# Half of g_attn moved from the attention's fill into the seven products behind it, softmax sums formed there, and new pacing constants

## The chip, the cores and the metric

The kernel runs on one core of a Trainium2 chip. The metric is the device time of one execution in microseconds (us). The engines named below are PE (matrix products), PEld (its weight loads), DVE (vector), ACT (scalar and activation functions), POOL (GpSimd) and SP (which issues most DMAs here). Each engine runs its own instructions in order and waits for the others by semaphores.

## The reference

One decoder block over 1040 positions (16 meta tokens and 1024 tokens), float32, 8 heads of 64:

```python
h = rmsnorm(x, norm_g)
proj = h @ w_in   # split: u_pool 512, z_pool 512, q, k, v 512 each, z_attn 512, f_logit 8, g_pool 1024, g_attn 1024
y_pool = causal_multiscale_pool(u_pool, pool_w, pool_scale) * silu(z_pool)
y_attn = forgetting_attention(q, k, v, log_sigmoid(f_logit + b_forget)) * silu(z_attn)
merged = sigmoid(g_pool) * (y_pool @ w_up_pool) + sigmoid(g_attn) * (y_attn @ w_up_attn)
out = rmsnorm(x + merged @ w_out, final_norm_g)   # only the 1024 tokens are returned
```

`forgetting_attention` is a causal softmax of `q k / 8` plus the summed log gates between key and query, times `v`.

## The kernel before

**Precision.** Matrix operands are kept as a high and a low part (`hh`/`hl` of the normed input, `whi`/`wlo` of weights). A product is three: high by high, high by low, low by high. Scores take two (L678, L679: `qa` and `ql` against `ka`), values two (L740: `ph` and `pl`, the parts of the probabilities). One half-chunk of a plain projection (128 columns by 512 tokens, 8 blocks of the contraction) is thus 24 matmuls of 128x512, all recorded at L170.

**Stages.** The input is normed and the first head pair's q, k, v are formed. Then comes the attention, then z_attn and z_pool, then the two up-projections with their gates, then the output product and the last norm.

**Attention.** Sixteen units follow each other: head pair p, head e, query half. A unit has 512 queries; with the first half it has 5 key blocks of 128 (units 0, 2, ... 14), with the second 9 (units 1, 3, ... 15). Per key block `qk` writes a score bank `ps` in PSUM (L678, L679), of which two exist; ACT empties it to `S` with the key's gate as bias (L687), DVE the masked part on the diagonal (L685), and DVE keeps the running maximum `pt` (L692; for the first block ACT copies it, L690). `maxes` then finds each query's maximum over the 128 partitions: transpose (L697), reduce (L702), two rounds of small ACT copies between partitions (L704, L707) with DVE maxima (L705, L708), and a transpose back (L710). `soft` handles a key block: DVE subtracts the maximum (L719), ACT takes the exp (L720) and rounds it to `ph` (L723), DVE forms the rest `pl` (L724), POOL adds the exps of all blocks up in `acc` (L732). `av` (L740) multiplies with V, two blocks behind. `finish` stores the unit's values; there DVE also transposes `acc` (L755) and reduces it (L757) to the sums of the softmax, which SP stores.

**Order.** The score products of the next unit are merged with the softmax of the present one (`merged`). Between them PE gets fill: projections that nothing in the attention waits for (u, the 8 chunks of g_pool, the 8 of g_attn, each chunk two half-chunks) and those that the next head pair wants (q, k, v). `F.pull(ns)` takes as many matmuls off the fill's list as fit into ns. How much is pulled is set by constants: behind each step `PACE` times an assumed DVE time less the step's PE time, `LM1` and `LM2` in `maxes`, and `LATENCY` ahead of each of a unit's last two value products.

```python
656:                yield w, 1.04 * w + 70, 2 * mm_ns(w), (lambda b=b: self.qk(b))
661:                yield w, 1.75 * w + 130, 2 * mm_ns(w), (lambda b=b: self.soft(b))
768:        for _, (w, dve, pe, f) in sorted(out_, key=lambda t: t[0]):
769:            f()
770:            F.pull(max(0.0, PACE * dve - pe))
```

So PE's order is that of the program text with the fill put in by these numbers. On the other engines a scheduler orders the instructions of this stage by what they depend on. What is left of the fill behind the last value product is done by `F.drain()` (L829). The evicted fill goes from PSUM through `st` (L342) to DRAM (`spill`) and returns for the gates.

**The seven products.** z_attn and z_pool are one product of the normed input with 1024 columns of `w_in`, done in the manner of Strassen: the input is cut in two token halves and two halves of the contraction, the weights in two halves of the contraction and the two column halves z_attn and z_pool. Seven products of block sums (512 by 512 by 512) replace eight. Each has four groups of 128 columns, each group is 12 matmuls (`g_prod`, L973). The block sums of the weights, `GS`, and of the input, `HS`, are made in DRAM during the attention: `put` (L586) is an SP DMA that copies, `add` a POOL DMA that accumulates, placed at units by the table `SUMS`. The first product's weights `graw` are loaded at unit 13 and rounded to `gw0` by ACT at unit 14 (L821), POOL forms the low part. In the product stage (manual order, `M2`) `w_split` makes the high part of each weight block on ACT (L953) and the low on POOL (L136) or DVE; `keep`, `plus_` and `silu` empty the banks on ACT and DVE. The up-projections (`up`) read the gates back from `spill` and take their sigmoid; the output product (L1232) is of the same kind as the seven.

## Time and profile before

| | us |
|---|---|
| median of 3 runs | 727.25 (726.98 to 727.72) |
| profiled execution | 727.18 |
| its span on the core | 725.5 |
| norm and first q, k, v (to the first score product) | 83.2 |
| attention (to the last value product) | 377.2 |
| rest of the fill | 12.6 |
| seven products | 82.0 |
| up-projections with gates | 87.0 |
| output product and last norm | 83.5 |

The stages are windows of the profiled execution, from 0 to 83.20, 460.40, 473.00, 555.00, 642.00 and 725.50 us. A row of the windows view gives for a stretch its length, the busy time of each engine with the number of instructions, the granted TensorE clock (1.00 is full), the DMA share and GB/s. A row of the timeline gives start, duration, engine, line, operation, result<-operands, shape, and in brackets how long the engine stood idle just before and what it waited for. A row of the chain of waits gives start, length and line of a piece of the work that ended last. A row of the groups (line, engine, operation, tiles, shape, count) gives busy time and mean ns of one, then the idle time ahead of them. In the list of PE's waits stand the tile and line that waited, what released it, and the sum, the number and the longest of the waits.

### The profile page before, as it was taken

Reading aid. Unit: us, or ns where it says so; the run is one execution under the profiler, and the core shown is the slowest. Engines: PE = TensorE matmul, PEld = TensorE weight load, DVE = VectorE, ACT = ScalarE, POOL = GpSimd, SP = SyncE. Lnnn points to the kernel's source line nnn. Section 1 sums busy time; section 2 is a strip of 40 time slices with the busy share of each in tenths; the row PEclk is TensorE's granted clock in tenths of the full one; section 3 lists DMA queues with packets and bytes.
Section 4 is the critical chain, followed back from the end, with each engine's and each line's share of the span. In section 5 each row is a group of like instructions: output and inputs, shape, how many; then the busy total and the mean of one; then the engine's idle time right before and its main releaser. Section 6 shows DMA issues by size and latency. Waiting matters only on the chain.

```text
span 725.5 us, 10804 instructions
## 1 busy us (share of the span) xinstructions
PE 712.8 (98%) x3637; PEld 613.8 (85%) x3637; DVE 506.9 (70%) x913; ACT 422.4 (58%) x930; POOL 330.8 (46%) x409
## 2 busy tenths in 40 slices
PE   8999999999999999999999999999999999999996
PEld 6997999998888898898888878888888888888885
DVE  5753577667688676886768658765877545888775
ACT  6652577557686677676765576252776423525445
POOL 5412236639446584463653666493843010006152
PEclk9999999999999999999999999999999999999998
DMA  9201124782984868838576599486906267761006
GB/s 307 63 26 34 29 84 166 175 262 60 295 201 95 222 173 221 218 90 222 104 202 148 156 265 248 126 301 202 293 12 238 93 219 248 248 245 59 0 2 232
DMA packets 88506, 119.40 MB, mean 165 GB/s; under 512 B 11297, under 2 KB 54305, under 8 KB 86450
## 3 DMA queue, kind: packets, MB, share of 16 engines
q1 hardware_dynamic: 84896, 99.83, 43.0%
q0 software_dynamic: 2256, 16.25, 12.4%
q10 hardware_dynamic: 1298, 2.63, 1.0%
q8 instruction: 28, 0.46, 0.3%
q14 instruction: 28, 0.23, 0.1%
HBM read 92.81 MB, written 53.67 MB: 202 GB/s over the span
## 4 chain that ended last, share of the span: by engine, by line
PE 84%; ACT 3%; DVE 2%; DMA 1%; POOL 1%; issue 1%; POOLq 0%; ACTq 0%; DVEq 0%
PE pj L170 53%; PE pj L1232 8%; PE pj L973 8%; PE po L740 5%; PE pt L973 3%; PE pt L1232 2%; PE ps L679 2%; PE ps L678 2%; PE pj L515 1%; DMA graw<-in_w_in_dram 1%; POOL acc L732 1%; ACT S L687 1%; DMA raw<-in_w_in_dram 1%; ACT S L720 1%; PE pj L300 0%
## 5 line engine op out<-in xcount | busy, mean ns | idle before, releaser
L170 PE MATMUL pj<-hh,whi 128*128 128x512 f32 (+3 forms) x640 | 144.9, 352 | 0.0
L170 PE MATMUL pj<-hh,wlo 128*128 128x512 f32 (+3 forms) x640 | 143.2, 350 | 0.3 <-POOL wlo L434 0.3
L170 PE MATMUL pj<-hl,whi 128*128 128x512 f32 (+3 forms) x640 | 141.9, 350 | 0.0
L158 POOL TENSOR_TENSOR wlo<-raw,whi 128x256 fp32r<-128x256 f32 x116 | 90.7, 826 | 84.4 <-ACT whi L156 33.1
L170 PEld LDWEIGHTS pj<-hh,whi 128*128 128x128 f32 x640 | 108.0, 188 | 12.1 <-ACT hh L223 0.5
L170 PEld LDWEIGHTS pj<-hl,whi 128*128 128x128 f32 x640 | 108.1, 188 | 12.0
L170 PEld LDWEIGHTS pj<-hh,wlo 128*128 128x128 f32 x640 | 108.0, 188 | 12.0 <-POOL wlo L434 0.5
L724 DVE TENSOR_TENSOR pl<-S,ph 128x512 fp32r<-128x512 f32 (+4 forms) x112 | 83.5, 756 | 26.6 <-ACT ph L723 25.7
L732 POOL TENSOR_TENSOR acc<-acc,S 128x272 f32<-128x272 f32 (+4 forms) x80 | 74.4, 930 | 14.5 <-ACT S L720 9.3
L692 DVE TENSOR_TENSOR pt<-pt,S 128x400 f32<-128x400 f32 (+2 forms) x96 | 46.8, 487 | 44.7 <-ACT S L687 43.1
L687 ACT ACTIVATE S<-ps,negc 128x400 f32<-128x400 f32 (+2 forms) x96 | 48.5, 514 | 37.0 <-DVE S L685 33.0
L136 POOL TENSOR_TENSOR gw<-graw,gw 128x256 fp32r<-128x256 f32 x40 | 45.5, 1173 | 29.8 <-ACT gw L953 12.2
L723 ACT ACTIVATE ph<-S 128x512 fp32r<-128x512 f32 (+4 forms) x112 | 52.7, 479 | 9.6 <-PE po L740 9.2
L720 ACT ACTIVATE S<-S 128x512 f32<-128x512 f32 (+4 forms) x112 | 49.8, 478 | 13.3 <-DVE S L719 13.2
L719 DVE TENSOR_TENSOR S<-S,pt 128x512 f32<-128x512 f32 (+4 forms) x112 | 50.7, 498 | 0.6
L1125 DVE TENSOR_TENSOR rl<-pj,rl 128x512 f32<-128x512 f32 x32 | 22.0, 690 | 28.7 <-PE pj L170 28.4
L973 PE MATMUL pj<-gh,gw 128*128 128x512 f32 x180 | 42.0, 389 | 0.0
L156 ACT ACTIVATE whi<-raw 128x512 fp32r<-128x512 f32 x58 | 33.8, 622 | 11.6 <-DMA raw<-in_w_in_dram 5.1
L973 PEld LDWEIGHTS pj<-gh,gw 128*128 128x128 f32 x180 | 33.8, 188 | 7.1
L678 PE MATMUL ps<-qa,ka 128*128 128x512 f32 (+4 forms) x112 | 36.5, 326 | 3.2 <-ACT S L687 3.2
L679 PE MATMUL ps<-ql,ka 128*128 128x512 f32 (+4 forms) x112 | 37.5, 335 | 0.0
L740 PE MATMUL po<-pl,V 128*128 128x512 f32 (+4 forms) x112 | 37.4, 334 | 0.0
(229 smaller groups left out, 1304.7 us busy)
## 6 DMA issues: line engine op xcount, KB each, us to landing
raw<-in_w_in_dram SPq DMA_DIRECT2D x31, 512.0 KB, 5.2
gs<-in_w_in_dram SPq DMA_DIRECT2D x5, 1024.0 KB, 9.9
td<-in_w_out_dram SPq DMA_DIRECT2D x5, 1024.0 KB, 8.4
xt<-in_x_dram SPq DMA_DIRECT2D x8, 512.0 KB, 7.4
sp_gp<-st SPq DMA_DIRECT2D x16, 256.0 KB, 4.6
gs<-gs POOLq DMA_DIRECT2D x4, 1024.0 KB, 9.1
td<-td POOLq DMA_DIRECT2D x4, 1024.0 KB, 11.3
sp_ga<-st SPq DMA_DIRECT2D x16, 256.0 KB, 4.4
```

The lines of the kernel that those rows point to most:

```text
L158: ins = nc.gpsimd.tensor_tensor(lo[:, k:k + 2], raw[:, k:k + 2], r32(hi[:, k:k + 2]), op=ALU.subtract)
L170: nc.tensor.matmul(ps, a, b, start=(i == 0), stop=(i == len(seq) - 1))
L678: nc.tensor.matmul(ps[:kb, c0:], ka[:, k0:k0 + kb], qa[:, q0 + c0:q0 + 512], start=True, stop=False)
L679: nc.tensor.matmul(ps[:kb, c0:], ka[:, k0:k0 + kb], ql[:, q0 + c0:q0 + 512], start=False, stop=True)
L687: nc.scalar.activation(s[:kb, f0:], ps[:kb, f0:], AF.Identity, bias=nb_)
L720: exps.append(nc.scalar.activation(s[:kb, c0:], s[:kb, c0:], AF.Exp))
L723: nc.scalar.activation(ph[:kb, c0:], s[:kb, c0:], AF.Copy)
L724: dves.append(nc.vector.tensor_tensor(pl[:kb, c0:], s[:kb, c0:], r32(ph[:kb, c0:]), op=ALU.subtract))
L732: accs.append(nc.gpsimd.tensor_tensor(acc[:kb, c0:], acc[:kb, c0:], s[:kb, c0:], op=ALU.add))
L740: nc.tensor.matmul(self.po[:, c0:], v, r[:kb, c0:], start=(b == 0 and i == 0), stop=(b == self.nb - 1 and i == 1))
L973: nc.tensor.matmul(ps, op_w[n][p][k // 2][:, k % 2, i * 128:(i + 1) * 128], op_h[n][q][k // 2][:, k % 2], start=start and m == 0, stop=m = ...
L1232: nc.tensor.matmul(ps, pick(A_, k, p)[:, i * 128:(i + 1) * 128], pick(B_, k, q)[:, c0:c1], start=start and n == 0, stop=n == 11, skip_grou ...
```

## The change

Chunks 4 to 7 of g_attn leave the fill. Chunks 4 and 5 are put beside z_attn, 6 and 7 beside z_pool, so that the column halves of the seven products are 768 wide in place of 512: six groups for each product, 42 in place of 28. The block sums `GS` become 512x768, each copied by two DMAs (`put_g`).

The weight blocks are now loaded in pairs of 128 columns (`pair_in`), and `w_split` makes one group's operand at a time: ACT the high part, and the low part POOL in two pieces for two groups of three and DVE in one for the third. A table `order` lists the 42 groups, and `before`/`extra` say what other work stands at which group. `evict` empties the banks; the new gate chunks are put together in two tiles `XE` and stored to `spill` as the others are (`g_store`, `g_flush`). Chunks 6 and 7 come out with the other sign, which `up` takes into its sigmoid by a scale of -1.

The sums of the softmax: `finish` no longer transposes and reduces `acc`; SP stores the whole `acc` (128x512, 256 KB a unit) to `accd`. In the product stage `acc_in` loads two units at a time and `acc_sum` transposes and reduces 1024 columns, eight times.

The pacing constants change as well: `PACE`, the assumed times of the steps, `LM2`, and `TAIL` in place of `LATENCY` ahead of a unit's last two value products.

```diff
-PACE = 1.67
+PACE = 1.0
 LATENCY = 1800.0
-LM1, LM2 = 1400.0, 3200.0
+LM1, LM2 = 1400.0, 1800.0
+TAIL = 900.0
...
+accd = dr.tile([128, 16, 512], F32, name="accd")
-GS = {n: dr.tile([512, 512], F32, name=f"gs{n}") for n in (1, 2, 3, 4, 5)}
+GS = {n: dr.tile([512, 768], F32, name=f"gs{n}") for n in (1, 2, 3, 4, 5)}
+def put_g(dst, src):
+    put(dst[:, :512], src[0])
+    put(dst[:, 512:], src[1])
...
-yield w, 1.04 * w + 70, 2 * mm_ns(w), (lambda b=b: self.qk(b))
+yield w, 1.05 * w + 165 + 300 * (b * KB + KB > self.t0), 2 * mm_ns(w), (lambda b=b: self.qk(b))
-yield w, 1.75 * w + 130, 2 * mm_ns(w), (lambda b=b: self.soft(b))
+yield w, 2.6 * w + 376, 2 * mm_ns(w), (lambda b=b: self.soft(b))
...
-at = ap_.tile([KB, 512], F32, name="mt")
-after(nc.vector.transpose(at, acc), dves[-1])
-r = sm.tile([128, 16], F32, name="sr")
-nc.vector.tensor_reduce(r, at.rearrange("p (j b) -> p j b", b=32), axis=AX.X, op=ALU.add)
-nc.sync.dma_start(sums[4 * self.p + 2 * self.e + self.half], r)
+nc.sync.dma_start(accd[:, 4 * self.p + 2 * self.e + self.half], acc)
...
-raws = [(n, j) for n, c in (("gp", 8), ("ga", 8)) for j in range(c)]
+raws = [(n, j) for n, c in (("gp", 8), ("ga", 4)) for j in range(c)]
...
-    F.pull(LATENCY)
+    F.pull(TAIL)
     u.av(b)
...
+def acc_in(k):
+    nc.sync.dma_start(zp[k % 2].rearrange("p (u c) -> p u c", u=2), accd[:, 2 * k:2 * k + 2])
+def acc_sum(k):
+    at = zp[2 + k % 2]
+    sall = XE[1][:, 0, :256].rearrange("p (u j) -> p u j", j=16)
+    nc.vector.transpose(at, zp[k % 2])
+    nc.vector.tensor_reduce(sall[:, 2 * k:2 * k + 2].rearrange("p u j -> p (u j)"),
+                            at.rearrange("p (j b) -> p j b", b=32), axis=AX.X, op=ALU.add)
...
+def w_split(e):
+    n, i = e
+    raw = raw_w[n, "aabbgg"[i]][:, :, 128 * (i % 2):][:, :, :128]
+    op = bp.tile([128, 2, 4, 128], F32R, name="gw", tag="y", bufs=6)
+    op_w[e] = op
+    nc.scalar.activation(op[:, 0], raw, AF.Copy)
+    if splits[0] % 3 == 2:
+        nc.vector.tensor_tensor(op[:, 1], raw, r32(op[:, 0]), op=ALU.subtract)
+    else:
+        for k in (0, 2):
+            nc.gpsimd.tensor_tensor(op[:, 1, k:k + 2], raw[:, k:k + 2], r32(op[:, 0, k:k + 2]), op=ALU.subtract)
+    splits[0] += 1
...
+order = [(n, i) for n in range(7) for i in {5: (3, 2, 1, 0, 4, 5), 6: (4, 5, 3, 2, 1, 0)}.get(n, range(6))]
...
+for x, e in enumerate(order[:38]):
+    if x == 0:
+        g_prod(order[0])
+        g_prod(order[1])
+    if 4 <= x + AH < 42:
+        split_next(order[x + AH])
+    if x + 2 < 38:
+        g_prod(order[x + 2])
+    for f in before.get(e, ()):
+        f()
+    if x:
+        evict(order[x - 1])
...
-    ins = nc.scalar.activation(sg_, sg_, AF.Sigmoid)
+    ins = nc.scalar.activation(sg_, sg_, AF.Sigmoid, scale=-1.0 if a and j > 5 else 1.0)
```

How this moves instructions is shown at three places. In these rows a line number is that of the program they belong to: the fill is L170 before and L171 after, the score products are L678 and L679 before, L691 and L692 after; `pj` is a bank of the fill, `ps` a score bank. The first place is PE from the last fill ahead of unit 9 to its first score product; of before:

```order
L300 MATMUL pj_3359<-ident_93,vt_3044 128x128 x4
L170 MATMUL pj_3383<-hh0_119,whi_3374 128x512 x4
L170 MATMUL pj_3383<-hh1_121,whi_3374 128x512 x4
L170 MATMUL pj_3383<-hl0_120,whi_3374 128x512 x4
L170 MATMUL pj_3383<-hl1_122,whi_3374 128x512 x4
L170 MATMUL pj_3383<-hh0_119,wlo_3375 128x512 x3
L678 MATMUL ps_3437<-qa_2363,ka_2528 128x512
```

The same place on PE after the change, from unit 8's last value product on (`po` with `ph` and `pl` is L753 there):

```order
L753 MATMUL po_3004<-ph_3189,V_1911 128x16
L753 MATMUL po_3004<-pl_3190,V_1911 128x16
L171 MATMUL pj_3225<-hh1_121,whi_3216 128x512 x3
L171 MATMUL pj_3225<-hl0_120,whi_3216 128x512 x4
L171 MATMUL pj_3225<-hl1_122,whi_3216 128x512 x4
L171 MATMUL pj_3225<-hh0_119,wlo_3217 128x512 x4
L691 MATMUL ps_3280<-qa_2279,ka_2452 128x512
```

Between unit 8's last score product and unit 9's first stand 23 matmuls of fill in place of 36; between those of units 6 and 7, 25 in place of 39.

The second place is PE from unit 9's first to its fourth score product; of before:

```order
L170 MATMUL pj_3383<-hh0_119,wlo_3375 128x512
L170 MATMUL pj_3383<-hh1_121,wlo_3375 128x512 x4
L170 MATMUL pj_3458<-hh0_119,whi_3374 128x512 x4
L678 MATMUL ps_3463<-qa_2363,ka_2528 128x512
L679 MATMUL ps_3463<-ql_2364,ka_2528 128x512
L170 MATMUL pj_3458<-hh1_121,whi_3374 128x512 x2
L678 MATMUL ps_3471<-qa_2363,ka_2528 128x512
L679 MATMUL ps_3471<-ql_2364,ka_2528 128x512
L170 MATMUL pj_3458<-hh1_121,whi_3374 128x512 x2
L170 MATMUL pj_3458<-hl0_120,whi_3374 128x512
L678 MATMUL ps_3479<-qa_2363,ka_2528 128x512
L679 MATMUL ps_3479<-ql_2364,ka_2528 128x512
```

The same place after the change:

```order
L171 MATMUL pj_3225<-hh1_121,wlo_3217 128x512 x4
L171 MATMUL pj_3300<-hh0_119,whi_3216 128x512 x3
L691 MATMUL ps_3304<-qa_2279,ka_2452 128x512
L692 MATMUL ps_3304<-ql_2280,ka_2452 128x512
L171 MATMUL pj_3300<-hh0_119,whi_3216 128x512
L691 MATMUL ps_3311<-qa_2279,ka_2452 128x512
L692 MATMUL ps_3311<-ql_2280,ka_2452 128x512
L171 MATMUL pj_3300<-hh1_121,whi_3216 128x512
L691 MATMUL ps_3317<-qa_2279,ka_2452 128x512
L692 MATMUL ps_3317<-ql_2280,ka_2452 128x512
```

Behind the first score product stand 7 matmuls of fill in place of 9, behind the second 1 in place of 2, behind the third 1 in place of 3.

The third place is ACT at the same time, where unit 8's exps (`S_3263` and `S_3320`, L720), their rounding (`ph`, L723) and the evictions of unit 9's first score banks (`S_3436`, L687) share the engine; of before:

```order
L309 ACTIVATE V_3046<-pj_3359 128x3x64
L723 ACTIVATE ph_3489<-S_3159 128x400
L720 ACTIVATE S_3263<-S_3263 128x272
L720 ACTIVATE S_3263<-S_3263 128x144
L309 ACTIVATE V_3046<-pj_3359 128x64
L723 ACTIVATE ph_3511<-S_3263 128x272
L720 ACTIVATE S_3320<-S_3320 128x16
L600 ACTIVATE neg_3629<-hh1_121 128x512
L687 ACTIVATE S_3436<-ps_3437,negc_116 128x512
L690 ACTIVATE pt_3435<-S_3436 128x512
L342 ACTIVATE st_3455<-pj_3383 128x512
L687 ACTIVATE S_3436<-ps_3463,negc_116 128x512
```

The same place after the change, where exps are L733, their rounding L736, evictions L700 and the first block's copy L703:

```order
L733 ACTIVATE S_3028<-S_3028 128x512
L736 ACTIVATE ph_3290<-S_3028 128x512
L733 ACTIVATE S_3028<-S_3028 128x400
L733 ACTIVATE S_3124<-S_3124 128x272
L736 ACTIVATE ph_3326<-S_3028 128x400
L700 ACTIVATE S_3279<-ps_3280,negc_116 128x512
L736 ACTIVATE ph_3348<-S_3124 128x272
L703 ACTIVATE pt_3278<-S_3279 128x512
L343 ACTIVATE st_3297<-pj_3225 128x512
L733 ACTIVATE S_3124<-S_3124 128x144
L700 ACTIVATE S_3279<-ps_3304,negc_116 128x512
```

The first eviction of unit 9 now stands ahead of unit 8's exps of 144 and 16 columns, and between the first and the second eviction stand four instructions in place of two. In the last unit the conversion to `gw0` stands ahead of the second eviction, where before it stood behind it.

More of the change, by code (lines that the diff above doesn't have):

```diff
@@ L979, in tile_hybrid_block, with g_prod @@
     T0_, T1_ = slice(0, 512), slice(512, 1024)
+    order = [(n, i) for n in range(7) for i in {5: (3, 2, 1, 0, 4, 5), 6: (4, 5, 3, 2, 1, 0)}.get(n, range(6))]
+    onto, banks = {}, [0]
+    def g_prod(e):
+        n, i = e
+        if i < 4 and n in (0, 2, 5, 6):
+            ps = ga_[i]
+        else:
+            ps = gb_[banks[0] % 4]
+            banks[0] += 1
+        onto[e] = ps
+        m, fresh = 0, i > 3 or n not in (2, 5, 6)
+        for p, q in ((0, 0), (0, 1), (1, 0)):
+            for k in range(4):
+                nc.tensor.matmul(ps, stat(n, i, p, k), op_h[n][q][k // 2][:, k % 2],
+                                 start=fresh and m == 0, stop=m == 11, skip_group_check=True)
+                m += 1
     def keep(dst, ps):
@@ L1000, in u_in @@
         nc.sync.dma_start(U[g], spill["u", g])
-    w_in_(1)
+    pairs = [(0, "g")] + [(n, q) for n in range(1, 7) for q in {5: "bag", 6: "gba"}.get(n, "abg")]
+    pair_in(*pairs.pop(0))
     u_in(3)
+    acc_in(0)
+    acc_in(1)
+    pair_in(*pairs.pop(0))
     h_in(2)
-    w_in_(2)
     u_in(2)
-    for k in range(2):
-        w_split(1, k)
     run(pool_chain(3))
@@ new lines, in tile_hybrid_block, with open_hq, pad_hq, steps_of @@
+    c0_ = pool_chain(0)
+    def open_hq():
+        nonlocal hq
+        HX.close()
+        hq = ctx.enter_context(tc.tile_pool(name="hq", bufs=8, side="right", reuse_waits="tile"))
+    def pad_hq():
+        hq.tile([128, SEQ], F32, name="wpad", tag="w")
+        hq.tile([128, SEQ], F32, name="pad", bufs=1)
+    def steps_of(g):
+        return lambda: next(g, None)
+    c2_, c1_ = pool_chain(2), pool_chain(1)
+    hq = None
+    before = {
+        (1, 3): [open_hq, lambda: h_split(2), lambda: h_in(4), lambda: pad_hq()],
+    }
@@ new lines, in tile_hybrid_block @@
+    AH = 4
+    for e in order[4:AH]:
+        split_next(e)
+    for x, e in enumerate(order[:38]):
[10 more added lines that the diff above has]
+            evict(order[x - 1])
+        if x % 3 == 2:
+            g_flush()
+        for f in extra.get(e, ()):
+            f()
```

251 lines of the change are left out of this document (127 added, 124 removed).

## The prediction

> **What bounds the kernel now.** First the page, for which engine is full, and the table of windows, for where.
>
> ```profile
> PE 712.8 (98%) x3637; PEld 613.8 (85%) x3637; DVE 506.9 (70%) x913; ACT 422.4 (58%) x930; POOL 330.8 (46%) x409
> ...
> PEclk9999999999999999999999999999999999999998
> ```
> ```profile
> core 0: us, PE busy (x) PEld busy (x) DVE busy (x) ACT busy (x) POOL busy (x), PEclk, DMA share, GB/s
> ...
> 83.20:460.40 377.20, 373.98 (x1958) 329.80 (x1956) 280.24 (x577) 250.63 (x630) 213.54 (x254) 1.00 0.66 174
> ...
> 473.00:555.00 82.00, 82.00 (x362) 67.60 (x362) 57.70 (x55) 44.39 (x60) 50.70 (x47) 1.00 0.59 190
> ```
>
> PE is busy in 98% of the span, at full granted clock. The first window runs from the first score product to the last attention value product, the second holds the seven products. PE is full in both; in the first DVE has 74% (280.24 of 377.20). So a removed matmul pays its issue interval, as long as nothing else then becomes late. The chain of waits gives that interval, and the list of PE's waits says how close the others are.
>
> ```profile
> 460.61 12.82 PE pj L170 x56
> ...
> 484.44 8.16 PE pj L973 x36
> ```
> ```profile
> PE ps L678 <- ACT S L687: 3.2, 6, 1.3
> ```
>
> 36 matmuls take 8.16 us, so one takes 226.7 ns and a product of 12 takes 2.72 us. The only repeated wait of PE is that of a score product (L678) for ACT to empty the score bank used two products earlier (L687). It occurs six times among 112 score products and costs 3.2 us in all, 1.3 at most.
>
> **The change: matmuls.** Eight half-chunks of g_attn with 24 matmuls each leave the attention (192, 43.5 us). Fourteen products with 12 each join the stage behind it (168, 38.1 us). The difference is 24 x 0.2267 = **-5.4 us**. This is certain while PE is full.
>
> The Trainium skill, "TensorE: Matmul & The Clock Gate", section "Wait — 56ns, not 53.3ns?", gives 215.7 ns between warm 512-wide matmuls. By it the gain would be 5.2; the trace's 226.7 decides.
>
> **The softmax sums** leave each unit's `finish` as two DVE instructions and come back in eight double-width pairs.
>
> ```profile
> L755 DVE STREAM_TRANSPOSE mt<-acc 128x512 f32<-128x512 f32 x16 | 11.4, 710 | 1.6
> L757 DVE TENSOR_REDUCE sr<-mt 128x16 f32<-128x512 f32 x16 | 10.9, 684 | 0.0
> ```
> ```profile
> 275.21 0.71 DVE L755 STREAM_TRANSPOSE mt<-acc 128x512 f32<-128x512 f32 x1
> 275.84 0.15 DVE L705 TENSOR_TENSOR pt<-pt,mx 128x16 f32<-128x16 f32 x1
> 275.95 0.69 DVE L757 TENSOR_REDUCE sr<-mt 128x16 f32<-128x512 f32 x1
> 277.48 0.17 DVE L708 TENSOR_TENSOR mz<-pt,my 128x16 f32<-128x16 f32 x1 [0.84 <-ACT my L707]
> ```
> ```profile
> 275.13 0.37 ACT L704 ACTIVATE mx<-pt 64x16 f32<-64x16 f32 x2 [2.42 <-DVE pt L702]
> 275.54 1.15 ACT L156 ACTIVATE whi<-raw 128x512 fp32r<-128x512 f32 x2
> ```
>
> They stand where DVE waits for ACT's small copies of the maxima anyway. ACT's copies end at 275.50 and L705 starts at 275.84, so of L755's 0.71 us about 0.25 to 0.3 is in the chain, and nothing of L757's. The 22.3 us of DVE work that leaves the attention therefore shortens a unit's chain by about 0.25 us only, though up to 1.4 where DVE has a queue. Behind the attention 22.3 us come back (the double-width forms have no row; twice these two is the estimate). That window has 57.70 busy of 82.00 on DVE and grows by 38.1, so the 22.3, plus fourteen evictions at an estimated 0.7 (the 512-wide rows above), still leave DVE near 75%. I cost this at nothing there; if the cover failed, each us of DVE excess would be a us of PE. On SP the store of `acc` replaces the store of the sums, and waits for the same last POOL add; the evicted fill behind it in SP's queue is no later than now: nothing.
>
> **The pacing** is where it turns. The order shows 13 fill matmuls fewer between unit 8's last score product and unit 9's first (23 for 36), and two fewer for each place between unit 9's second and fourth. The rows of before for this place, PE then ACT:
>
> ```profile
> 272.78 0.17 PE L678 MATMUL ps<-qa,ka 128*128 128x16 f32 x1
> ...
> 282.39 0.40 PE L678 MATMUL ps<-qa,ka 128*128 128x512 f32 x1
> ...
> 286.99 0.40 PE L678 MATMUL ps<-qa,ka 128*128 128x512 f32 x1
> ```
> ```profile
> 279.17 1.06 ACT L720 ACTIVATE S<-S 128x512 f32<-128x512 f32 x2 [0.25 <-DVE S L719]
> ...
> 283.70 0.68 ACT L687 ACTIVATE S<-ps,negc 128x512 f32<-128x512 f32 x1
> ...
> 285.58 0.69 ACT L687 ACTIVATE S<-ps,negc 128x512 f32<-128x512 f32 x1
> ```
>
> Now PE needs 9.61 us from the last score product of unit 8 (272.78) to the first of unit 9 (282.39), and ACT's first exp of unit 8 starts 6.39 after the former. PE arrives 3.2 us after the exps began, when ACT has nearly done them. With 13 matmuls fewer (2.95 us) PE arrives after 6.66. The exp now starts at about 5.5: by the order the two conversions of weights (1.15) no longer stand between the small copies, whose second pair they hold back by some 0.65, and L755 is gone (0.25). So PE arrives 1.2 us behind the first exp. The fourth score product then comes 3.5 later (4.60 from 282.39 to 286.99, less five matmuls), at exp + 4.65. It needs the second eviction. By ACT's new order that stands behind three exps and two copies (2.2 us at the spacing of such rows), the first eviction (0.7), four small ones of the old and new unit (an estimated 1.5; of before 1.2 lie between the two evictions, 283.70 + 0.68 to 285.58) and itself (0.7): exp + 5.1. **PE waits 0.5 us.**
>
> For unit 7 the same with its own rows:
>
> ```profile
> 226.46 0.17 PE L678 MATMUL ps<-qa,ka 128*128 128x16 f32 x1
> 226.60 0.37 PE L740 MATMUL po<-ph,V 128*128 128x272 f32 x1
> ...
> 236.32 0.39 PE L678 MATMUL ps<-qa,ka 128*128 128x512 f32 x1
> ```
> ```profile
> 233.44 1.06 ACT L720 ACTIVATE S<-S 128x512 f32<-128x512 f32 x2 [1.10 <-DVE S L719]
> 234.40 1.04 ACT L723 ACTIVATE ph<-S 128x512 fp32r<-128x512 f32 x2
> ```
>
> 14 matmuls fewer: PE arrives 9.86 - 3.17 = 6.7 after unit 6's last score product, the exp starts 6.98 - 0.25 = 6.7 after it; the fourth product wants exp + 3.5, the eviction ends at exp + 5.3: 1.8 us. I take the mean, 1.2, for the six units 3 to 13 that have nine key blocks: 7.2 us. Bounds: 0 (if ACT is faster) and 1.8 each, so 0 to 11.
>
> The last unit has a load in that queue.
>
> ```profile
> 427.73 1.06 ACT L821 ACTIVATE gw<-graw 128x1024 fp32r<-128x1024 f32 x1 [2.52 <-DMA graw<-in_w_in_dram]
> ```
> ```profile
> 429.42 0.51 PE L678 MATMUL ps<-qa,ka 128*128 128x512 f32 x1 [1.29 <-ACT S L687]
> ```
>
> ACT stands still 2.52 us for the weights of the first product, and PE 1.29. In the new order this conversion is ahead of the second eviction, not behind it. I take 2.0, bounds 1.3 to 4. Together 9.2. From that go the waits which before has at such places: this 1.29, and
>
> ```profile
> 147.17 0.50 PE L678 MATMUL ps<-qa,ka 128*128 128x512 f32 x1 [0.69 <-ACT S L687]
> ```
> ```profile
> 333.63 0.50 PE L678 MATMUL ps<-qa,ka 128*128 128x512 f32 x1 [0.30 <-ACT S L687]
> ```
>
> so **+6.9 us** (bounds -2.3 to +13).
>
> **Where DVE is full.** The q and k projections of the next head pair are evacuated while units 5 and 9 run.
>
> ```profile
> 203.50:226.60 23.10, 23.10 (x131) 21.26 (x129) 21.21 (x39) 19.13 (x46) 16.27 (x19) 1.00 0.45 100
> ```
> ```profile
> 225.79 0.75 DVE L724 TENSOR_TENSOR pl<-S,ph 128x272 fp32r<-128x272 f32 x1
> ...
> 317.75 0.53 DVE L724 TENSOR_TENSOR pl<-S,ph 128x272 fp32r<-128x272 f32 x1
> ```
> ```profile
> 201.33 0.33 PE L678 MATMUL ps<-qa,ka 128*128 128x144 f32 x1 [0.55 <-ACT S L687]
> ...
> 319.05 0.37 PE L740 MATMUL po<-ph,V 128*128 128x272 f32 x1
> ```
>
> DVE is 92% busy and unit 5's seventh value product (226.60, quoted above) starts 0.06 us after its operand is done (225.79 + 0.75). From the last score product to there PE loses nine fill matmuls by the order (2.0 us). DVE saves 0.25 to 1.4, so PE waits 0.6 to 1.7 us; I take 1.2, less 0.55 that it loses at 201.33 now. Unit 9's seventh has 0.77 us to spare (319.05 less 318.28) and loses an estimated 2.2: 0 to 1.2, I take 0.6. Together **+1.2**.
>
> **Sum**: 727.18 (the profiled execution, 725.5 span and 1.7 around it; the median of the runs, 727.25, is the same) - 5.4 + 6.9 + 1.2 = **729.9 us**.
>
> **The rivals.** *The full gain.* ACT gets through exps and evictions sooner than I add up, so that the second eviction ends within 3.5 us of the unit's first score product. For it: only six of 112 score products wait there now, and ACT is only 66% busy (250.63 of 377.20). Against: the order is fixed, and ACT cannot pass an exp. It decides when the eviction comes 0.5 to 1.8 us earlier. Time: 727.2 - 5.4 = 721.8, to 725.5 with some waits left.
>
> *Transfers.* The sum tables grow by half and 4 MB of `acc` are stored while the attention gets shorter.
>
> ```profile
> 422.00:428.00 6.00, 6.00 (x27) 4.70 (x26) 0.88 (x2) 3.09 (x6) 3.05 (x5) 1.00 1.03 318
> ```
> ```profile
> gs<-in_w_in_dram SPq DMA_DIRECT2D x5, 1024.0 KB, 9.9
> ```
>
> The DMA engines are already full when the first product's weights come. A 1.5 MB table takes up to 14.9 us at this rate, and a late weight load stops ACT and with it PE: two loads 2 us later each give 734.
>
> *The seven products become bound by POOL or DVE.*
>
> ```profile
> L136 POOL TENSOR_TENSOR gw<-graw,gw 128x256 fp32r<-128x256 f32 x40 | 45.5, 1173 | 29.8 <-ACT gw L953 12.2 <-DMA sp_y<-t 10.5 <-PE pt L973 7.0
> ```
>
> Two such subtractions belong to a tile on POOL, two tiles in three: 4.7 us in 8.2 of PE. It would need a missed product of 2.7 in every third group to matter; one or two give 733 to 735.
>
> *The clock.* If the last unit's wait outgrew what the throttle allows, PE would run on at a lower clock; no window shows that, with waits to 1.3 us (clock 1.00). The time would be that of the forecast and a few us of slower matmuls: 731.6. The Trainium skill, the same page, section "HAM oscillation — how this bites in real kernels", sets the limit at idle gaps over about 3.4 us, which is a rule against thinning the fill; a window of that length at half clock would cost 1.7.
>
> **How the numbers follow.** Forecast case 0.46 (own range 725.5 to 734), full gain 0.34, transfers 0.10, products bound 0.06, clock 0.04. 0.2% of 727.25, about what a measurement here can tell from no change, is 1.45. Of the forecast case 0.01 lies below 725.8, 0.17 within it and 0.28 above 728.7. So faster 0.35, same 0.17, slower 0.48. The range 721.5 to 735 takes in the full gain, and leaves the worst transfers and bounds out.
>
> **What will show it.** The seven products' stretch should grow from 82 to 120 us without a wait of PE. The attention stretch (377.20 us up to the last value product) should lose 192 matmuls less the nine of the drained rest (41.5) and win back some 8, so about 344. The wait of the score product for ACT's eviction should rise from 3.2 us to about 10, in one place of each long unit; a wait of value products for `pl` should appear at units 5 and 9. If the former stays near 3, the main step is wrong and the time falls to 722 to 725. Waits on raw loads, or in the product stage, would mean that I put the loss in the wrong stage.

## The result, and the profile after

| | median of runs, us | ratio to before (95%) |
|---|---|---|
| before | 727.12 (4 runs) | |
| after | 754.9 (752.88 to 757.81, 4 runs) | 1.0385 (1.0342 to 1.0427) |

The change makes the kernel 27.8 us slower. The profiled execution is the slowest of the four (757.81, span 756.1); before it was 727.18 (span 725.5), so the profiles are 30.6 us apart. The windows below cut the profile of after at its first score product, its last value product, its first product and its first up-projection; the columns are those of the same view before.

```profile
core 0: us, PE busy (x) PEld busy (x) DVE busy (x) ACT busy (x) POOL busy (x), PEclk, DMA share, GB/s
82.90:435.70 352.80, 338.03 (x1775) 297.71 (x1773) 264.70 (x544) 242.00 (x615) 200.36 (x236) 0.99 0.73 196
435.70:446.50 10.80, 10.80 (x51) 8.96 (x50) 6.20 (x5) 2.29 (x4) 5.09 (x5) 1.00 0.65 205
446.50:585.90 139.40, 127.15 (x530) 100.76 (x529) 92.27 (x96) 57.61 (x91) 58.46 (x70) 0.96 0.61 191
585.90:756.10 170.20, 163.49 (x733) 135.66 (x731) 116.36 (x173) 77.62 (x137) 35.77 (x57) 0.99 0.47 163
```

PE, all but full before in the attention and in the products, now is not: 338.03 of 352.80 in the attention, 127.15 of 139.40 in the products. No engine took its place (DVE 92.27, ACT 57.61, POOL 58.46 of the 139.40), so the loss is latency in chains, not work. What lies behind the products takes as long as it did.

The balance, from the starts of PE's rows: attention and rest of the fill took 390.0 us and take 363.6. The 192 matmuls that left are worth 43.5, so 17.1 are lost there. The products took 81.9 and take 139.4, 57.5 more, where the 168 new matmuls are worth 38.1: 19.4 lost. -43.5 + 38.1 + 17.1 + 19.4 = 31.1, of the 30.6 seen.

PE's waits of after:

```profile
PE ps L691 <- ACT S L700: 14.1, 9, 6.5
PE pj L171 <- DVE gx L1027: 7.2, 1, 7.2
PE pj L1016 <- ACT gw L973: 2.4, 2, 1.5
PE pj L1016 <- DVE gx L1027: 1.5, 1, 1.5
PE pn L415 <- DVE car L551: 1.3, 1, 1.3
PE pj L1016 <- DVE zp L1027: 1.2, 1, 1.2
```

The first row is the wait that was 3.2 before (L691 is the old L678). It nearly halves without its longest, 6.5. The next three rows with `gx` and `gw`, and the last, are in the product stage, where PE was busy throughout before. The longest one in the attention, in the timeline of PE and then of ACT:

```profile
404.40 0.79 PE L691 MATMUL ps<-qa,ka 128*128 128x512 f32 x1 [6.55 <-ACT S L700]
```
```profile
402.71 1.06 ACT L830 ACTIVATE gw<-graw 128x1024 fp32r<-128x1024 f32 x1 [5.76 <-DMA graw<-in_w_in_dram]
403.68 1.25 ACT L700 ACTIVATE S<-ps,negc 128x512 f32<-128x512 f32 x2
```

The conversion of the first product's weights stands ahead of the last unit's score evictions, and ACT waits 5.76 us for its load (2.52 before). The DMA view of 386 to 404 us shows this load's time from issue to landing, the last column, beside the accumulations in DRAM that POOL issued just before:

```profile
td<-td POOLq DMA_DIRECT2D x1, 1024.0 KB, 7.9
graw<-in_w_in_dram SPq DMA_DIRECT2D x2, 512.0 KB, 10.2
```

Before, the same view of 412 to 432 us has 6.6 for the two `graw` loads. What the product stage waits for is seen in the list of waits of ACT, which is in order:

```profile
ACT gw L973 <- DMA graw<-gs: 19.0, 5, 11.4
ACT gw L973 <- DMA graw<-in_w_in_dram: 12.5, 5, 4.3
ACT zp L1024 <- POOL zp L137: 12.1, 4, 3.7
ACT zp L1024 <- DVE zp L1027: 11.5, 4, 6.0
```

31.5 us (19.0 + 12.5) for raw weights, 23.6 for adds of z_pool by POOL and DVE that its silus need. Behind each of these waits stand evictions and weight splits. The loads are late for several reasons. SP issues one when its buffer is free, and of these there are two. SP's queue in the list of waits:

```profile
SPq L961 <- DVE gw L975: 23.7, 6, 7.7
SPq L961 <- POOL gw L978: 13.7, 8, 4.4
SPq L961 <- ACT gw L973: 12.7, 5, 3.9
```

These rows show for SP's loads of weights (L961) the readers of the old weights for which the buffer was not free. But the longest wait, the 11.43 us below, has more behind it. The rows are SP's, then POOL's and ACT's:

```profile
471.29 0.37 SPq L961 DMA_DIRECT2D graw<-gs  x1
...
482.49 0.36 SPq L961 DMA_DIRECT2D graw<-gs  x1
...
483.50 0.38 SPq L940 DMA_DIRECT2D sums<-ge  x1
488.89 1.93 SPq L944 DMA_DIRECT2D fin<-sums  x4
...
492.71 0.43 SPq L961 DMA_DIRECT2D graw<-gs  x1
```
```profile
481.03 1.44 POOL L978 TENSOR_TENSOR gw<-graw,gw 128x256 fp32r<-128x256 f32 x2 [1.29 <-ACT gw L973]
```
```profile
500.67 0.63 ACT L973 ACTIVATE gw<-graw 128x512 fp32r<-128x512 f32 x1 [11.43 <-DMA graw<-gs]
```

The load at 482.49 goes out when POOL's split of the pair loaded at 471.29 ends (482.47). In the program of the change these two loads, one behind the other, have the same buffer; in all its other loads of pairs the two buffers alternate. Behind it SP stores the finished sums and stands until they have landed, since it loads them back next (`L944 <- DMA sums<-ge`, 4.9 us in its list of waits). The next load of weights stands behind that in SP's queue and goes out at 492.71.

The last wait of the stage, 7.2 us, is one of PE for a bank that DVE has not emptied (timeline, PE's row and then DVE's):

```profile
566.32 0.79 PE L171 MATMUL pj<-plh,pwh 128*128 128x512 f32 x1 [7.21 <-DVE gx L1027]
```
```profile
564.97 0.69 DVE L975 TENSOR_TENSOR gw<-graw,gw 128x512 fp32r<-128x512 f32 x1 [2.25 <-ACT gw L973]
565.58 0.68 DVE L1027 TENSOR_TENSOR gx<-pj,gx 128x512 f32<-128x512 f32 x1
```

And behind waits PE runs at half clock for a while, as the windows view of after shows (the third column from the end is the clock):

```profile
226.00:229.00 3.00, 1.94 (x6) 1.25 (x6) 1.86 (x4) 2.86 (x7) 2.43 (x4) 0.76 1.00 218
229.00:232.00 3.00, 3.00 (x13) 2.72 (x12) 1.40 (x3) 1.81 (x3) 1.97 (x3) 0.67 1.09 216
404.00:408.00 4.00, 3.60 (x9) 2.83 (x10) 2.10 (x3) 3.56 (x6) 4.00 (x7) 0.50 0.12 47
566.00:573.00 7.00, 6.68 (x17) 5.22 (x18) 2.72 (x5) 0.63 (x1) 5.57 (x8) 0.55 0.23 75
```

The granted clock is 0.50 to 0.76 in these windows. The loss can be split by the time from each 512-wide matmul to the next start, less 0.2267: counted as waiting from 0.445 us on, as half clock from 0.33, as a slow interval below. The limits are chosen, so a short wait counts as half clock too.

| us lost | waits | half clock | slow interval |
|---|---|---|---|
| attention before | 2.6 | 0.6 | 5.1 |
| attention after | 14.6 | 3.1 | 6.3 |
| products before | 0.0 | 0.0 | 0.3 |
| products after | 13.5 | 3.0 | 3.2 |

### The profile page after: what moved, and what is told of

Its sections match the earlier page's. It is cut to its first block, busy times and chain, and to the rows that moved or that the text cites. A ratio compares the mean times of both kernels' runs of the same rounds, so it can differ in the third digit from the quotient of the medians.

```text
span 756.1 us, 10866 instructions
## 1 busy us (share of the span) xinstructions
PE 720.1 (95%) x3613; PEld 613.7 (81%) x3613; DVE 522.1 (69%) x917; ACT 425.5 (56%) x944; POOL 328.5 (43%) x417
## 3 DMA queue, kind: packets, MB, share of 16 engines
q0 software_dynamic: 2512, 18.35, 12.9%
## 5 line engine op out<-in xcount | busy, mean ns | idle before, releaser
L171 PE MATMUL pj<-hh,whi 128*128 128x512 f32 (+3 forms) x576 | 130.1, 353 | 0.2 <-DVE V L311 0.2
L171 PE MATMUL pj<-hh,wlo 128*128 128x512 f32 (+3 forms) x576 | 129.6, 348 | 0.1
L171 PE MATMUL pj<-hl,whi 128*128 128x512 f32 (+3 forms) x576 | 128.6, 346 | 0.0
L171 PEld LDWEIGHTS pj<-hh,whi 128*128 128x128 f32 x576 | 98.3, 192 | 10.8 <-PE pj L301 0.4
L171 PEld LDWEIGHTS pj<-hh,wlo 128*128 128x128 f32 x576 | 96.3, 189 | 9.3 <-POOL wlo L435 0.3
L159 POOL TENSOR_TENSOR wlo<-raw,whi 128x256 fp32r<-128x256 f32 x100 | 75.5, 794 | 64.9 <-ACT whi L157 25.4
L171 PEld LDWEIGHTS pj<-hl,whi 128*128 128x128 f32 x576 | 96.0, 188 | 8.8
L1016 PE MATMUL pj<-gh,gw 128*128 128x512 f32 x276 | 66.8, 397 | 5.0 <-ACT gw L973 2.4
L700 ACT ACTIVATE S<-ps,negc 128x400 f32<-128x400 f32 (+2 forms) x96 | 48.7, 515 | 33.2 <-DVE S L698 31.5
L1016 PEld LDWEIGHTS pj<-gh,gw 128*128 128x128 f32 x276 | 51.5, 188 | 19.0 <-ACT gw L973 3.7
L736 ACT ACTIVATE ph<-S 128x512 fp32r<-128x512 f32 (+4 forms) x112 | 52.4, 480 | 8.8 <-PE po L753 7.7
L733 ACT ACTIVATE S<-S 128x512 f32<-128x512 f32 (+4 forms) x112 | 50.1, 478 | 10.6 <-DVE S L732 10.5
L691 PE MATMUL ps<-qa,ka 128*128 128x512 f32 (+4 forms) x112 | 37.9, 338 | 14.3 <-ACT S L700 14.1
L973 ACT ACTIVATE gw<-graw 128x512 fp32r<-128x512 f32 x38 | 23.3, 624 | 39.7 <-DMA graw<-gs 19.0
L691 PEld LDWEIGHTS ps<-qa,ka 128*128 128x128 f32 x112 | 21.4, 191 | 21.2 <-ACT S L700 18.9
L692 PE MATMUL ps<-ql,ka 128*128 128x512 f32 (+4 forms) x112 | 38.1, 340 | 0.0
## 6 DMA issues: line engine op xcount, KB each, us to landing
td<-in_w_out_dram SPq DMA_DIRECT2D x5, 1024.0 KB, 12.9
```

What stands on the lines that cost most here:

```text
L159: ins = nc.gpsimd.tensor_tensor(lo[:, k:k + 2], raw[:, k:k + 2], r32(hi[:, k:k + 2]), op=ALU.subtract)
L171: nc.tensor.matmul(ps, a, b, start=(i == 0), stop=(i == len(seq) - 1))
L691: nc.tensor.matmul(ps[:kb, c0:], ka[:, k0:k0 + kb], qa[:, q0 + c0:q0 + 512], start=True, stop=False)
L700: nc.scalar.activation(s[:kb, f0:], ps[:kb, f0:], AF.Identity, bias=nb_)
L733: exps.append(nc.scalar.activation(s[:kb, c0:], s[:kb, c0:], AF.Exp))
L736: nc.scalar.activation(ph[:kb, c0:], s[:kb, c0:], AF.Copy)
```

## The experiments

Three theories for the products: A, the ring of two raw buffers makes the weights late; B, the sums of the softmax do (loads, DVE's work); C, the order of evictions, silus and splits on ACT and DVE is too serial. For the attention: the pacing constants, and the load of the first product's weights. Each run's stages, from the starts of PE's rows (first score product, last value product, first product, first up-projection, last matmul):

| run | median | attention | rest of fill | products | behind |
|---|---|---|---|---|---|
| before | 727.1 | 377.1 | 12.9 | 81.9 | 163.2 |
| after | 754.9 | 352.7 | 10.9 | 139.4 | 163.3 |
| e1 | 743.8 | 352.4 | 54.4 | 82.1 | 163.2 |
| e2 | 748.8 | 343.3 | 10.9 | 139.6 | 163.3 |
| e3 | 748.8 | 352.8 | 10.9 | 130.1 | 163.2 |
| e4 | 749.5 | 352.9 | 10.9 | 132.4 | 163.3 |
| e5 | 739.5 | 345.0 | 10.9 | 129.7 | 163.2 |
| e6 | 742.9 | 351.2 | 4.7 | 133.0 | 163.2 |
| e7 | 738.3 | 346.5 | 10.9 | 127.4 | 163.2 |
| e8 | 732.8 | 344.8 | 4.7 | 128.5 | 163.2 |
| e9 | 732.4 | 344.9 | 4.7 | 126.0 | 165.9 |
| e10 | 738.5 | 354.8 | 0.1 | 127.1 | 164.4 |
| e11 | 737.5 | 366.6 | 34.9 | 82.0 | 163.2 |
| e12 | 726.5 | 345.3 | 4.7 | 121.0 | 164.4 |
| e13 | 726.5 | 344.0 | 5.6 | 121.0 | 164.4 |
| e14 | 750.8 | 354.1 | 10.9 | 130.7 | 163.2 |
| e15 | 727.8 | 347.7 | 3.4 | 121.0 | 164.4 |
| e16 | 732.1 | 345.7 | 3.4 | 127.5 | 164.4 |

42 products and 24 matmuls of the pool mixing between them are 119.7 us if PE never waits.

**e1: the pacing alone.**

```diff
-PACE = 1.67
+PACE = 1.0
-LM1, LM2 = 1400.0, 3200.0
+LM1, LM2 = 1400.0, 1800.0
+TAIL = 900.0
...
```

> The kernel before with only the new pacing constants (PACE, the assumed step times, LM2, TAIL); all of g_attn stays in the fill, the sums stay in finish. The fill that is not pulled goes to the drain, so the number of matmuls is that of before. My step on the pacing says 6.9 + 1.2: about 735, with PE's waits for ACT's eviction (L687) up from 3.2 to about 10 us. The rival, that the new constants cost nothing and the attention's loss comes from the transfers alone, says 727.

743.77 (ratio 1.0231, 1.0211 to 1.025): 16.7 us for the constants alone, all in attention and rest of the fill (406.8 for 390.0), the number of matmuls unchanged. Two rows of the list of PE's waits of e1:

```profile
PE ps L679 <- ACT S L688: 10.1, 10, 1.8
PE po L741 <- ACT ph L724: 2.0, 1, 2.0
```

The eviction waits are the 10 us foreseen, 6.9 more than before. What was not foreseen is how much comes with them: waits of value products in the last unit, and the clock. Behind this pair of waits (PE's timeline of e1, then its windows),

```profile
310.44 0.50 PE L679 MATMUL ps<-qa,ka 128*128 128x512 f32 x1 [1.60 <-ACT S L688]
...
312.39 0.79 PE L679 MATMUL ps<-qa,ka 128*128 128x512 f32 x1 [0.76 <-ACT S L688]
```
```profile
308.00:312.00 4.00, 2.02 (x8) 1.03 (x6) 3.54 (x10) 3.92 (x9) 3.40 (x5) 0.96 1.08 223
312.00:315.00 3.00, 2.61 (x6) 2.13 (x7) 2.87 (x5) 2.55 (x7) 2.49 (x4) 0.50 0.93 232
315.00:318.00 3.00, 3.00 (x8) 2.32 (x8) 0.49 (x2) 1.11 (x2) 0.40 (x2) 0.50 0.41 132
```

PE was busy for 2.02 of 4 us, and then ran at clock 0.50 for 6. By the split above e1's attention loses 4.7 us to half clock and 11.8 to waits of 512-wide matmuls.

**e2: the first product's weights converted behind the last unit's scores.**

```diff
-        if i == 14:
+        if i == 15:
             g_w0 = ...
```

> The changed kernel, with the conversion of the first product's weights emitted at unit 15 in place of 14, so that it stands behind the last unit's score evictions on ACT. Theory: the 6.7 us wait of PE at 404 us and the 2 us at half clock behind it go, 754.9 - 8.7 = 746, and nothing later moves. Rival: the late table only moves the wait to the first product, 753 to 755.

748.82 (1.0308, 1.0279 to 1.0338). The attention is 9.4 us shorter, the products are the same, and in e2's list of PE's waits there is left for the score products

```profile
PE ps L691 <- ACT S L700: 7.7, 9, 1.6
```

The wait did not only move: the theory holds for it. The medians differ by 6.1, the profiled runs by 9.4; runs of after spread by 5 us. Of the 9.4 the last unit has 8.0; 0.8 is at 226 to 235 us, where after ran at half clock and e2 did not.

**e3 and e4: the sums, and a third buffer.** e3 forms the sums in `finish` as before. e4 keeps them and has:

```diff
-        raw_w[n, q] = wp.tile([128, 4, 256], F32, name="graw", tag="raw")
+        pool, tag = (gp, "g") if len(raw_w) in (2, 5, 8, 11) else (wp, "raw")
+        raw_w[n, q] = pool.tile([128, 4, 256], F32, name="graw", tag=tag)
...
+    pair_in(*pairs.pop(0))
```

> The changed kernel, with the softmax sums formed in finish again as before (16 x 512 columns), and no accd store, loads or sums in the product stage. The product stage takes 139.5 us in the changed kernel, 119.7 if PE never waited (42 x 2.72 and 24 x 0.227). Theory A (two buffers for the raw weights, each load waits for the pair before last): the stage still loses 10 us or more, over 130. Theory B (the sums' loads, DVE work and SP waits hold up the weights): the stage falls below 126, and the total to about 742.

> The changed kernel, with four of the nineteen weight pairs (the third, sixth, ninth and twelfth) loaded into a buffer of another pool, and one pair more loaded ahead of the stage. Theory A: ACT's waits for graw (31.5 us in all) fall by more than half, and the stage of 139.5 to 128 or less, total about 743. Theory C (the order of evictions and silus on ACT, DVE and POOL is too serial even with the weights there): the stage stays above 133.

748.77 and 749.52: the stage falls to 130.1 and 132.4. Neither theory has it alone: each edit removes all of PE's waits in the middle of the stage (13.5 us of waits become 7.4 and 8.2), and in both the long wait ahead of the first pool product stays (5.6 and 6.3). ACT's waits for raw weights fall from 31.5 us to 5.3 and 3.8. So it takes both, two buffers and the sums in this stage, to make the weights so late that PE waits. Both totals miss their forecasts of about 742 and 743.

**e14: the loads of the sums without the work.** e3 with the stores of `acc` and the eight 512 KB loads put back, no transposes or reductions of what they bring.

> e3 (sums formed in finish), with the accd stores and the eight 512 KB loads of the changed kernel put back, without the transposes and reductions that read them. e3's product stage was 130.1 with PE at 227 ns a matmul, e2's and e4's 232 to 233. If the slow interval comes with the loads, the stage loses 3 us to it here; if it comes with DVE's 1024-wide work, it stays at 0.6. And if the late weights come of the loads, PE's waits for the banks and gw in the middle of the stage (5.7 us in the changed kernel, none in e3) return.

750.75 (1 round), the stage 130.7, one short wait (0.2) in its middle, ACT's waits for `graw` 6.2 us. The loads are not it. What remains of B is three things that no run here takes apart. One is DVE's work: it splits the weights of every third group, and in the changed kernel that split stands behind transposes and reductions of 1.24 and 1.22 us (DVE's timeline of after):

```profile
475.24 1.24 DVE L934 STREAM_TRANSPOSE zp<-zp 128x1024 f32<-128x1024 f32 x1
476.51 1.22 DVE L935 TENSOR_REDUCE ge<-zp 128x32 f32<-128x1024 f32 x1
477.65 0.68 DVE L975 TENSOR_TENSOR gw<-graw,gw 128x512 fp32r<-128x512 f32 x1
```

The others are the two found above. The split at 477.65 freed its buffer at 478.33, but the load at 482.49 waited for the other one, and the buffer that was free got its load only at 492.71, behind SP's wait for the stored sums. In e3 and e14, where two loads in turn never have one buffer and the sums are stored in the attention, the same two loads go out 29.1 and 38.3 us (e3) and 29.1 and 39.6 us (e14) behind the first product, in after 36.0 and 46.2. Why the program of the change places this one load so was not tried.

**e5 to e8: the faults mended together.** All have e2's edit, and the two g_attn groups of the sixth product first in it, with the extras beside them moved:

```diff
-order = [... {5: (3, 2, 1, 0, 4, 5), 6: (4, 5, 3, 2, 1, 0)} ...]
+order = [... {5: (4, 5, 3, 2, 1, 0), 6: (4, 5, 3, 2, 1, 0)} ...]
```

e5 has e4's buffer, e7 has e3's sums; e6 and e8 are these with LM2 2400.

> e2 and e4 together, and the end of the product stage in another order: the two g_attn groups of the sixth product first in it, and the norms, silus and the last split of the pool moved so that they no longer stand between products and the evictions of banks. Theory C (PE's wait of 6 to 7 us ahead of the first pool product is a bank whose eviction DVE reaches late, behind its waits for ACT): the product stage falls from 132.4 (e4) to about 123, attention is 343 as in e2, total 749.5 - 9.4 - 9 = 731. Rival: the wait is for the pool chain itself (plh, pll) or for up weights and only moves, stage 130, total 738.

> e5 with LM2 2400 in place of 1800: about 27 of the 47 matmuls left for the drain go between a unit's maxima and the next unit's first score product. Theory (PE's waits in the attention are at a unit's first score products, for evictions that stand behind exps on ACT): waits for L700 fall from 7.7 by some 4 us and the half-clock stretches behind them go, total 4 to 6 below e5. Rival: ACT and DVE bound the long units, and the matmuls moved only shift the wait within the unit: no gain over 1 us.

> As e5, but with the sums formed in finish (e3) in place of the third raw buffer. If the sums and the missing buffer are two ways to the same stall, the product stage is that of e5 within 2 us; and if the steady matmul interval of 232 ns goes with the sums (as e3's records say: 0.6 us lost to it there, 3.3 in e4), the stage is 3 us shorter than e5's. Attention about 345: DVE has 22 us more there.

> e7 with LM2 2400: as e6 against e5, 4 to 6 us less than e7 by the theory, no gain by the rival. It would come to 722 to 726, and be the version that beats the kernel before, if both the theory of the ring and that of the unit starts hold.

739.52, 742.87, 738.3 and 732.77. e5 misses its 731: the stage is 129.7, not 123. The wait ahead of the pool product is now for another bank (3.5 us, `st` for `gx`): it moved by one eviction, which fits a DVE that is late as such. e7's stage is 2.3 shorter than e5's, where 3 was foreseen from the matmul interval. LM2 2400 gained 5.5 in e8 and lost 3.4 in e6. By the table e6 gains nothing in attention and rest of the fill (355.9 in both; waits of 1.0 and 2.2 us met at 228 to 231 us, and the clock fell behind them), and its products are 3.3 longer, with a new wait of 2.8 for a bank of `zp`. These runs alone do not settle where the attention's waits come from.

**e9 to e11.** e9 puts each of the last four products ahead of its pool product, e10 adds LM2 2800, e11 is e1 with LM2 3200 as before.

> e8, and at the end of the product stage each of the last four products stands ahead of the pool product of its row, the last norm and the pool's last split behind the first of them. Theory C (the wait ahead of the pool product is DVE's lateness at the banks, e8: 5.6 us and some 2 at half clock): with two products' time more for DVE and three of its instructions out of the way the wait falls below 1.5 us, the stage from 128.5 to 122, the total from 732.8 to 726. Rival: DVE and ACT lose the time a step later, at the first up-projections, and the total stays above 731.

> e9 with LM2 2800: no fill is left for the drain. By the theory of the unit starts PE's waits for L700 (5.3 us in e8) fall to 3 or less, which is 2 to 3 us below e9. Rival: the last units want the fill that is now gone, the value products and the first product wait, and the total is not below e9's.

> The kernel before with the new pacing constants, but LM2 as it was (3200): the 1.4 us of fill ahead of each unit's first score product come back. e1 took 743.8. Theory (my step: the loss of the pacing is at the unit starts, where the evictions stand behind the exps): waits for L687 fall from 10.1 to below 4 and the total to 730 or less. Rival (the thinner fill inside the units costs as much): above 737.

732.44: the rival was right, the time is lost a step later (the stage is 2.5 shorter, what lies behind 2.7 longer). 738.48: with no fill left the last value products wait 3.0 us for ACT and half clock follows. 737.47: e11 has 11.9 us of eviction waits, more than e1; 5.4 of these are the last unit's again (its load, with 1.8 us of half clock behind). The rest is 6.5, where e1 has 8.4 without its last unit. So the fill ahead of a unit's first score product does not cure it, and the rival of e11 came out, though only just (above 737); that the rest lies between the first score products, where two or three matmuls fewer no longer cover an eviction, is what e13 tries.

**e12: the silus one eviction later.**

```diff
     def evict(e):
+        while late_:
+            z_ = late_.pop(0)
+            silu(z_, z_, -1.0)
...
-                silu(zp[i][:, T0_], zp[i][:, T0_], -1.0)
+                late_.append(zp[i][:, T0_])
```

> e9, with the silus of z_pool each one eviction later on ACT (behind the DVE and POOL adds that they need) and the last pair of rc loads behind the first norm on SP. Theory: at the end of the product stage DVE and ACT are late because ACT, in order, waits for POOL's and DVE's adds of z_pool (about 3.5 us each time) with the weight splits behind it; then PE's waits there (7.6 us with the half clock in e9) fall below 3 and the total from 732.4 to 728 or less. Rival: the lateness is the raw weights' and the rc loads' (ACT waits for graw 2.65 and 2.9 us there), and the silus only swap one wait for another: above 731.

726.53 (1.0003, 0.9993 to 1.0013). The stage falls from 126.0 to 121.0, and its window has PE busy for all but 0.7 us:

```profile
432.60:553.60 121.00, 120.30 (x530) 98.94 (x528) 78.97 (x82) 57.69 (x91) 70.46 (x72) 1.00 0.59 182
```

This fits theory C for the end of the stage: ACT stood in order behind adds of DVE and POOL, 18.5 us in e9 (10.3 and 8.2) and 6.7 in e12. But e12 also moves the last loads of `rc`: in e9 SP waited 5.9 us to issue them, with a load of weights behind, and in e12 it does not. The two are not taken apart. ACT still waits 6.0 us once for a raw weight there, and PE no longer notices.

**e13, e15, e16.** e13 adds one fill matmul behind a long unit's second to fourth score products (LM2 2000); e15 a second in units 3, 7 and 11; e16 is e15 with the sums behind the attention, as the change has them, and e4's buffer.

> e12 with one fill matmul more behind each of the second to fourth score products of a unit with nine key blocks, and LM2 2000 in place of 2400, so that the fill left for the drain is about the same. Theory: part of the loss in the attention is between the first score products themselves, where two or three matmuls less no longer cover an eviction (the wait comes at the fourth product); then PE's waits for L700 (5.4 us) fall by 2 or more. Rival: they grow, since less fill stands ahead of the first score product.

> e13, with a second matmul of fill at the same three places in units 3, 7 and 11, where PE's waits for L700 are now (3.9 us in e13). Theory of e13 (waits between the first score products): they fall below 2.5 and the total by 1 to 2, to 725, below the kernel before (726.4). Rival: no change within 0.5 us.

> e15, but with the sums in the product stage as in the change, and the third raw buffer of e4. This is the whole change with its faults mended. Theory: DVE's 22 us less in the attention are worth what e2 and e7 differ by there (343.3 against 346.5, 3 us), and DVE's sums cost the product stage 3 us by the slower matmul interval (e5 against e7): total within 1.5 us of e15. Rival: the sums' work still makes the weights late, the stage is above 127 and the total above 731.

726.54, 727.83 and 732.13. The eviction waits fall from 6.0 (e12) to 3.9 in e13, but the total does not move, and e15 has 4.5: other places (value products, DVE) begin to wait. e16 says what the moved sums are worth by themselves: the attention is 2.0 shorter than e15's, the products are 6.5 longer. Taking them out of the attention loses some 4 us even with the buffer and the order mended; ACT still waits 9.0 us at once for weights there, and SP 3.3 for the stored sums. No version beat the kernel before; e12 and e13 equal it.

## Why the prediction was wrong

**The matmuls** were right: 24 fewer, -5.4, and PE's full stages behind and in e12's products show each of them paid at 226.7 ns.

**The eviction waits** were right in kind and nearly in size. For units 3 to 13 the prediction has 6 x 1.2 = 7.2; e2, where the load is out of the way, has 6.0 there. It has 1.56 more at unit 1, which the prediction left at nothing. Evenly spread it is not: units 7 and 11 have 2.4 and 2.0, unit 3 has 0.1. The prediction put the wait at each unit's fourth product; in units 7 and 11 it is at the third too. With the load out of the way the attention takes 343.3 us, where 344 was foreseen. Two slips change little: the lower bound of the term is -1.0 (0 + 1.3 - 2.3), not -2.3, and the `exp + 5.3` of unit 7 has no sum behind it.

**The last unit** was mis-sized: "I take 2.0, bounds 1.3 to 4"; it was 6.5, with 1.6 us lost to half clock behind. That the conversion stands ahead of the second eviction was right; the load took 10.2 us where it took 6.6 before. The rival of the transfers had this mechanism, as two loads 2 us later each, but not its cause: in e1 and e11, with the old tables and no stores of `acc`, the two loads take 9.1 to 10.7 us as well, so the new constants are enough for it. Why the load is slower beside the same accumulations was not tried.

**The product stage** is the step that failed: "I cost this at nothing there", because DVE would be busy to 75%. DVE's work came out as foreseen (92.27 us, where 57.7 + 22.3 + 9.8 is 89.8), but the stage was longer, so it was busy to 66% only, and the stage lost 19.4: 13.5 in waits, 3.0 at half clock, 3.2 in the slow interval. What the runs showed in the place of that step are late weights in the middle (gone in e3 and e4) and evictions that come late at the end (gone with e12's edits). A share of busy time cannot show the latency of a hand-written order. Part of it is in the diff: two buffers for 256 columns of raw weights, where before a whole product's weights were loaded at once, into several pools; and sums that SP stores and waits for ahead of weights. The rival that came nearest asked for a missed product in a group, at 0.06. The prediction named the sign itself: waits in the product stage would mean that it had put the loss in the wrong stage.

**The clock**: the prediction weighed the Trainium skill, "TensorE: Matmul & The Clock Gate", section "HAM oscillation — how this bites in real kernels", with its limit of idle gaps over about 3.4 us, and gave a case at 731.6 with chance 0.04. Two of after's stretches at half clock go with waits above it, of 6.55 and 7.21 us; there the trace agrees. But the runs also show half clock behind pairs of waits well below it (1.60 and 0.76 in e1; 1.32 and 1.06 in after at 226 to 229), so the gap rule as stated does not bound it. By the split half clock cost 6.1 us in the profile of after (3.1 + 3.0), short waits included, most of it behind the two long waits. In e2 the like pair at 226 us (1.29 and 1.08) is followed by no such stretch, so which runs it hits differs; that would also fit after's spread of 5 us, but this was not tried.

**Value products at units 5 and 9**: 1.2 foreseen, 0.2 measured.

## What to carry to other kernels

Fill that covers an engine's latency is not free to move: when 192 of its matmuls left the attention and the pacing was cut, PE waited for ACT, although ACT and DVE were busy for only 69 and 75% of it, and a transfer that had been almost hidden came out. In a stage with a hand-written order, count for each ring of buffers the time from the last read of a buffer to the first use of its next load, look up which buffer a load really takes, and ask on each in-order engine, SP too, what stands behind a wait; a busy share of 66% says nothing of these. An instruction that waits for two other engines (the silu behind two adds) is worth trying one step later in the order.

## What the runs showed of the hardware

The interval of the same 128x512 matmuls has two steady values. In e3 and e14 36 of them take 8.16 us (start to start), 226.7 ns; in the changed kernel 8.40:

```profile
480.04 8.56 PE L1016 MATMUL pj<-gh,gw 128*128 128x512 f32 x36
488.44 2.96 PE L1016 MATMUL pt<-gh,gw 128*128 128x512 f32 x12
```

That is 233.3 ns, in single intervals of 229 and 238 in turn for 45 us, at clock 1.00 in the records. It costs some 3 us of the stage in each of the runs whose sums are formed there (after, e2, e4, e5, e6, e16) and 0.4 to 0.6 in those without (e3, e7 to e10, e12 to e15). The runs without have it as well, but mostly in the first 12 us or so of the stage: in e3 it falls to 226.7 at 458 us, 12 us behind the first product. So the longer stay goes with sums formed in the stage, not with their loads (e14), yet it lasts after the transposes and reductions have ended (481 us in after). What holds it is open.

The stretches at half clock up to the end of the products last one, two or three times 3.4 us in after and e1. The windows view gives a clock of 0.50 or 0.51 for 227.6 to 231.0 us (3.4 us), 401.6 to 408.5 (6.9) and 562.1 to 572.3 (10.2) of after, and 0.50 for 311.7 to 318.5 (6.8) and 407.3 to 410.7 (3.4) of e1.
